# A decoder block on one core: weights repacked into load order, two more Strassen chunks, block sums and pooling products issued later

## The chip, the core and the metric

The kernel runs on one core of a Trainium2 chip. The metric is the time of one execution on the device in microseconds (us); a median of several runs is compared. The engines are TensorE (PE, with its weight loads as PEld), VectorE (DVE), ScalarE (ACT), GpSimd (POOL) and SyncE (SP, which here only issues DMAs).

## The reference

One decoder block for a sequence of T = 256 rows of D = 2048 features, all float32. A normalized input `z` is projected once by `w_in` (2048 x 11280); the result is split into the inputs of a pooling mixer, of a chunked gated linear attention (GLA) and of two branch gates.

```python
z = rms_norm(x, norm_mix_pre)
p, q, k, v, low, r, gates = split_combined(z @ w_in)     # 1024, 1024, 1024, 2048, 16, 2048, 2 x 2048
y = pool_mixer(p, w_pool, pool_scale)     # per group: trailing mean (window 2, 4, 8, 16) minus token, then 256 x 256
o = rms_norm_per_head(gla_chunked(q, k, v, log_a)) * silu(r)
ga, gb = sigmoid(gates + b_branch_gates)
m = ga * (y @ w_branch_a) + gb * (o @ w_branch_b)
x = x + rms_norm(m @ w_out, norm_mix_post)
h = rms_norm(x, norm_ffn_pre)
f = silu(h @ w_ffn_gate) * (h @ w_ffn_up)                # 5632 wide
out = x + rms_norm(f @ w_ffn_down, norm_ffn_post)
```

(The names are shortened; the arithmetic is that of the reference.) Nearly all work is the product of 256 rows with some 280 MB of weights, each of which is read once.

## The kernel before

**Jobs, steps and units.** Every weight matrix is cut into chunks of 512 output columns (CW). One chunk is a `Job` (L207); the list of jobs stands at L876 to L913 in the order of computing: p (2 chunks), r (4; the first is 528 wide and takes the 16 columns of `low` along), q and k (2 each), branch_a (4), v (4), gates (8), branch_b (4), out (4), and then the FFN in three parts of up to four chunks: gate and up alternating, then down (4). A `Step` is 256 weight rows of a chunk, loaded as one `raw` of 512 KB from SyncE's queue (L256). A *unit* is a step or a part (below) with its matmuls; the loop at L978 issues one unit after another, and this loop is what sets the order on every engine.

**Precision.** A weight tile is split into a high half `wh` (ScalarE, L265) and a low half `wl` = raw - wh (VectorE, L269), and each product takes three matmuls: high x high (L296), high x low (L297), low x high (L298). A step is 12 matmuls of 512 columns. Jobs p, q and k are computed transposed ("across", L285 to L287, 24 matmuls of 256 columns a step).

**Strassen chunks.** A job with `fast=True` computes its first eight 128-row weight tiles (two block rows of 512 KB x 2) by a Strassen-Winograd scheme in seven `Part`s of 12 matmuls with 256 columns (L357 to L359), and the rest, four steps for a 2048-row weight, as before. Its weight blocks are loaded at L943 into `blocks` tiles. Sums of weight blocks are made in place: part r5 by an accumulating DMA from GpSimd's queue (L329), q6, q7 and q4 on VectorE (L318, L320, L322); parts are split at L333 (ScalarE) and L337 (VectorE). Parts q1, r5, q6, q7 are "early": `merged` (L231) puts them between the last units of the job before. Two subtractions on 256 columns (L369) finish the products. Before the change 39 chunks are Strassen chunks: gates 1, 3, 5, 7, branch_b 1, 3, out 1, 2, and in the FFN gate and up chunks except number 0, and down except the last.

**Block sums of activations.** A Strassen chunk needs sums of the activations' blocks too, once for each activation (h, o, m, h2, f of each part). `combine` (L173) returns them as six pieces with 12 operations on VectorE (L182, L188, L193; 128 x 512 each) and four on ScalarE (L187).

**What sets the order.** `prepare_to` (L946) runs loads, block sums and splits for the next units: up to BUFS = 4 splits ahead of TensorE; raws in RAWS = 3 buffers, blocks in BLOCKS = 3. Small work is queued in `bg`; the loop takes one entry after each unit (L994). `after(n, f)` (L375) puts work into `soon`, which is looked at before each unit (L982): entries run while the *first* of them is due, so an entry that is not due holds up those behind it. At the end of an up chunk (L827) f = silu(gate) * up is made; after chunk 1 of a part the six pieces of `combine` go to the front of `bg` three units later, one per unit from there; the two transposes of f's halves (`to_operand`, after 1 and 2 units) stand behind that entry in `soon`.

**Pooling mixer.** `pool_group` (L450) runs from `bg` for each of four groups: running sums on VectorE, then the load of the group's `w_pool` (ScalarE's queue, L467), four matmuls (L471) and the split into `yT`, all at once.

## Time and profile before

| | |
|---|---|
| median of 3 runs | 1521.74 us (1520.41 to 1523.68) |
| profiled execution | 1520.68 us, span 1518.9 us |
| TensorE busy | 98% of the span |
| VectorE, ScalarE, GpSimd busy | 77%, 58%, 5% |
| read from device memory | 282.74 MB, 188 GB/s over the span |
| clock granted to TensorE | 0.998 of full speed |

A row like `L337 DVE TENSOR_TENSOR wl<-blocks,wh ... x273 | 331.7, 1221 | 79.6 <-ACT wh L333 76.5` is a group of instructions: line, engine, operation, output <- inputs by the program's names, shape, count, then busy us and mean ns of one, then the engine's idle time just before these instructions and what ended most of it. A row of a window gives start and end in us, its length, each engine's busy us (and count), the granted clock, the mean share of DMA engines in use and GB/s. In a timeline each row is a start, a duration, an instruction, and in brackets the idle time before it with what ended it. Ends of matmuls are modelled, so that a run of short matmuls is better read by its count in a full window than by the duration of one.

### The profile page before, as it was taken

The page shows a single profiled execution, that of the slowest core. Times are in us where ns is not written, and L with a number is a line of the kernel's source. Part 1 is how long each engine was busy: PE and PEld are TensorE (multiplying, and loading weights), DVE is VectorE, ACT ScalarE, POOL GpSimd, SP SyncE. Part 2 cuts the span into 40 slices and gives each one's busy share as a digit, 9 for nine tenths or more (in the row PEclk, how much of TensorE's full clock was granted, in tenths as well). Part 3 has the DMA queues.
Part 4 walks back from the last instruction along what each step waited for, and adds up shares of the span by engine and source line. Part 5 has one row for each costly group of instructions (what it writes and reads, how often), then busy time and mean ns, then how long its engine had stood idle before and what let it go on. Part 6 is the DMA issues. An engine that isn't in the chain of part 4 may idle for free.

```text
span 1518.9 us, 22882 instructions
## 1 busy us (share of the span) xinstructions
PE 1487.0 (98%) x8904; PEld 1306.4 (86%) x8904; DVE 1173.0 (77%) x1303; ACT 879.3 (58%) x1136; POOL 80.3 (5%) x89
## 2 busy tenths in 40 slices
PE   8999999999999999999999999999999999999997
PEld 8888999888888888888878989998998889888886
DVE  5665445785578866787768899888889898888997
ACT  6367333555455555554656666666666666666663
POOL 2000000000000000000000000000000000000001
PEclk9999999999999999999999999999999999999999
DMA  9856665445547776657865777778876777787664
GB/s 293 241 158 194 193 182 179 126 137 155 166 125 221 236 236 196 213 168 255 259 184 153 213 196 231 218 225 224 236 212 199 226 217 222 226 236 222 186 181 139
DMA packets 167630, 306.79 MB, mean 202 GB/s; under 512 B 9773, under 2 KB 30977, under 8 KB 167265
## 3 DMA queue, kind: packets, MB, share of 16 engines
q1 hardware_dynamic: 144176, 279.15, 57.7%
q0 software_dynamic: 22128, 24.92, 10.7%
q8 instruction: 70, 1.15, 0.3%
q10 hardware_dynamic: 1216, 1.25, 0.3%
q14 instruction: 40, 0.32, 0.1%
HBM read 282.74 MB, written 2.10 MB: 188 GB/s over the span
## 4 chain that ended last, share of the span: by engine, by line
PE 80%; DVE 10%; issue 4%; DMA 4%; ACT 2%; POOL 0%; SPq 0%; DVEq 0%; ACTq 0%; POOLq 0%
PE acc L296 16%; PE acc L297 16%; PE acc L298 16%; PE ac L358 4%; PE ac L357 4%; PE ac L359 4%; PE acc L358 3%; PE acc L357 3%; PE acc L359 3%; DVE wl L269 3%; PE acc L287 2%; PE acc L286 2%; PE acc L285 2%; DMA raw<-in_w_in_dram 2%; DVE wl L337 2%
## 5 line engine op out<-in xcount | busy, mean ns | idle before, releaser
L269 DVE TENSOR_TENSOR wl<-raw,wh 128x1024 fp32r<-128x1024 f32 (+1 forms) x364 | 444.6, 1223 | 211.5 <-ACT wh L265 209.5
L265 ACT ACTIVATE wh<-raw 128x1024 fp32r<-128x1024 f32 (+1 forms) x364 | 385.0, 1059 | 382.0 <-PE acc L298 171.3
L337 DVE TENSOR_TENSOR wl<-blocks,wh 128x1024 fp32r<-128x1024 f32 x273 | 331.7, 1221 | 79.6 <-ACT wh L333 76.5
L333 ACT ACTIVATE wh<-blocks 128x1024 fp32r<-128x1024 f32 x273 | 286.6, 1058 | 139.7 <-PE acc L298 62.8
L329 POOL DMA_DIRECT2D blocks<-blocks x39 | 50.7, 1301 | 792.4 <-DMA blocks<-in_w_ffn_gate_dram 163.1
L359 PE MATMUL ac<-wh,x 128*128 128x256 f32 x312 | 87.3, 280 | 0.0
L357 PE MATMUL ac<-wh,x 128*128 128x256 f32 x312 | 87.2, 279 | 0.0
L358 PE MATMUL ac<-wl,x 128*128 128x256 f32 x312 | 87.1, 279 | 0.0
L297 PE MATMUL acc<-wl,h22h 128*128 128x512 f32 x176 | 69.9, 397 | 5.2 <-DVE wl L269 5.2
L296 PE MATMUL acc<-wh,h22h 128*128 128x512 f32 x176 | 69.8, 397 | 0.2 <-ACT wh L265 0.2
L298 PE MATMUL acc<-wh,h23l 128*128 128x512 f32 x176 | 69.3, 394 | 0.0
L297 PE MATMUL acc<-wl,h23h 128*128 128x512 f32 x176 | 69.3, 394 | 0.0
L296 PE MATMUL acc<-wh,h23h 128*128 128x512 f32 x176 | 69.2, 393 | 0.0
L298 PE MATMUL acc<-wh,h22l 128*128 128x512 f32 x176 | 69.2, 394 | 0.0
L357 PEld LDWEIGHTS ac<-wh,x 128*128 128x128 f32 x312 | 58.6, 188 | 2.6
L358 PEld LDWEIGHTS ac<-wl,x 128*128 128x128 f32 x312 | 58.6, 188 | 2.4
L359 PEld LDWEIGHTS ac<-wh,x 128*128 128x128 f32 x312 | 58.8, 189 | 0.3 <-DVE x L188 0.2
L297 PE MATMUL acc<-wl,h3h 128*128 128x512 f32 (+1 forms) x128 | 49.8, 389 | 0.9 <-DVE wl L269 0.9
L296 PE MATMUL acc<-wh,h2h 128*128 128x512 f32 (+1 forms) x128 | 49.9, 390 | 0.0
L297 PE MATMUL acc<-wl,h2h 128*128 128x512 f32 (+1 forms) x128 | 49.7, 388 | 0.0
L298 PE MATMUL acc<-wh,h3l 128*128 128x512 f32 (+1 forms) x128 | 49.7, 388 | 0.0
L298 PE MATMUL acc<-wh,h2l 128*128 128x512 f32 (+1 forms) x128 | 49.7, 388 | 0.0
(540 smaller groups left out, 4123.6 us busy)
## 6 DMA issues: line engine op xcount, KB each, us to landing
raw<-in_w_in_dram SPq DMA_DIRECT2D x152, 512.0 KB, 3.7
raw<-in_w_ffn_gate_dram SPq DMA_DIRECT2D x48, 512.0 KB, 4.9
raw<-in_w_ffn_up_dram SPq DMA_DIRECT2D x48, 512.0 KB, 4.5
blocks<-in_w_ffn_down_dram SPq DMA_DIRECT2D x44, 512.0 KB, 5.0
raw<-in_w_ffn_down_dram SPq DMA_DIRECT2D x44, 512.0 KB, 4.9
blocks<-in_w_ffn_gate_dram SPq DMA_DIRECT2D x40, 512.0 KB, 4.8
blocks<-in_w_ffn_up_dram SPq DMA_DIRECT2D x40, 512.0 KB, 4.8
blocks<-blocks POOLq DMA_DIRECT2D x39, 512.0 KB, 6.7
```

Source lines behind the costliest of these rows:

```text
L265: act.activation(self.hi[self.s], self.raw, AF.Copy)
L269: dve.tensor_tensor(self.lo[self.s], self.raw, f32(self.hi[self.s]), op=ALU.subtract)
L285: pe.matmul(dst, wh, ah, start=first and c % 2 == 0, stop=False)
L296: pe.matmul(ps, ah, hi[:, i, cs], start=first, stop=False, skip_group_check=j.fast)
L297: pe.matmul(ps, ah, lo[:, i, cs], start=False, stop=False, skip_group_check=j.fast)
L298: pe.matmul(ps, al, hi[:, i, cs], start=False, stop=last, skip_group_check=j.fast)
L329: pool.dma_start(self.block((0, 1)), self.block((0, 0)), accum_op=ALU.add)
L333: act.activation(self.hi, self.src, AF.Copy)
L337: dve.tensor_tensor(self.lo, self.src, f32(self.hi), op=ALU.subtract)
L357: pe.matmul(dst, ah, wh, start=i == 0 and p in ("q1", "r5"), stop=False, skip_group_check=True)
L358: pe.matmul(dst, ah, wl, start=False, stop=False, skip_group_check=True)
L359: pe.matmul(dst, al, wh, start=False, stop=i == 3 and p in EARLY, skip_group_check=True)
```

## The change

1. **Layout.** The host lays the seven big weights out as one-dimensional arrays in load order: each 512 KB load is contiguous, 4 KB for each of the 128 partitions (before: two rows of 2 KB). A pair of block loads now brings the left and the right 256 columns of four weight tiles (before: two tiles of 512 columns each), so each block is contiguous in its `blocks` tile. `w_pool` is laid out likewise. The `raw`, `wh` and `wl` tiles have the width of the job instead of 528 columns.
2. **Block sums of f.** The six pieces go out 5 units apart in FFN parts 0 and 1, and 2 units apart in part 2, starting at the next unit, through `after`. `soon` is now a list in which each due entry runs, whatever stands ahead of it.
3. **Pooling product.** The load of `w_pool`, the four matmuls and the split of y come three units after the group's differences.
4. **Strassen chunks.** Gates 2, 4, 5, 6, 7 (before 1, 3, 5, 7) and out 0, 1, 2 (before 1, 2): 41 instead of 39.

```diff
+WEIGHTS = ("w_in", "w_branch_a", "w_branch_b", "w_out", "w_ffn_gate", "w_ffn_up", "w_ffn_down")
...
+        yield "gates", n, "w_in", 0, kt, OFF_GA + n * CW, CW, n in (2, 4, 5, 6, 7)
+    for n in range(4):
+        yield "b", n, "w_branch_b", 0, kt, n * CW, CW, n in (1, 3)
+    for n in range(4):
+        yield "out", n, "w_out", 0, kt, n * CW, CW, n < 3
...
+def packed(name, w):
...
+    out = []
+    for _, _, which, k0, kt, c0, width, fast in plan():
+        if which != name:
+            continue
+        rows = w[0, k0 * P:(k0 + kt) * P, c0:c0 + width].reshape(kt, P, width)
+        if fast:
+            for b in range(2):
+                blocks = rows[b * 4:b * 4 + 4].reshape(4, P, 2, HW)
+                out.append(blocks.transpose(2, 1, 0, 3).ravel())
+            rows = rows[4 * FAST:]
+        out.append(rows.reshape(-1, GK, P, width).transpose(0, 2, 1, 3).ravel())
+    return np.concatenate(out)
...
+        def combine_slowly(self, first, step):
+            for i, f in enumerate(self.combine()):
+                after(first + i * step, f)
...
         def load(self):
             j = self.j
-            r0 = (j.k0 + self.g * GK) * P
-            raw = wp.tile([P, GK, CW + RANK], F32, tag="raw", name=nm("raw"), bufs=RAWS)
-            s = self.s = (slice(None), slice(None), slice(0, j.width))
-            sync.dma_start(raw[s], j.w[r0:r0 + GK * P, j.c0:j.c0 + j.width].rearrange("(g p) c -> p g c", p=P))
-            self.raw = raw[s]
+            n = GK * P * j.width
+            self.raw = wp.tile([P, GK, j.width], F32, tag="raw", name=nm("raw"), bufs=RAWS)
+            sync.dma_start(self.raw, j.w[j.at + self.g * n:j.at + (self.g + 1) * n]
+                           .rearrange("(p g c) -> p g c", p=P, g=GK))
...
-            rows, cols_ = which
-            return self.j.blocks[rows][:, :, cols_ * HW:(cols_ + 1) * HW]
+            return self.j.blocks[which[0]][:, which[1]]
...
-                    bg.popleft()()
+                    (bg.popleft() if bg else soon.pop(0)[1])()
...
-    soon = deque()
+    soon = []
...
+        after(3, lambda: pool_product(g, d))
+
+    def pool_product(g, d):
         wt = two(scratch())
-        act.dma_start(wt, w_pool[0, g].rearrange("(k p) c -> p k c", p=P))
+        act.dma_start(wt, w_pool[g])
...
-                after(3, lambda: bg.extendleft(reversed(fa[part].combine())))
+                after(3, lambda: fa[part].combine_slowly(0, 5 if part < 2 else 2))
...
-            project(OFF_GA + which * D, n, gate_done(which, n), fast=n % 2 > 0)
-        jobs.append(Job(w_branch_b[0], lambda: oT["o"], KT, n * CW, yb_done(n), fast=n % 2 > 0))
-        jobs.append(Job(w_out[0], lambda: mix["m"], KT, n * CW, out_done(n), tail=3 * (n == 3), fast=n in (1, 2)))
...
+    for kind, n, name, k0, kt, c0, width, fast in plan():
+        jobs.append(Job(source[name], at[name], kt, width, fast, **kinds[kind](n)))
+        at[name] += kt * P * width
...
-            tile_ = blk.tile([P, 4, CW], F32, tag="blocks", name=nm("blocks"))
+            tile_ = blk.tile([P, 2, 4, HW], F32, tag="blocks", name=nm("blocks"))
             j.blocks.append(tile_)
+            n = 4 * P * HW
             for i in range(2):
-                r0 = (j.k0 + rows_ * 4 + i * 2) * P
-                sync.dma_start(tile_[:, i * 2:i * 2 + 2], j.w[r0:r0 + 2 * P, j.c0:j.c0 + CW]
-                               .rearrange("(g p) c -> p g c", p=P))
+                at = j.at + (rows_ * 2 + i) * n
+                sync.dma_start(tile_[:, i], j.w[at:at + n].rearrange("(p k c) -> p k c", p=P, k=4))
...
-        while soon and soon[0][0] <= 0:
-            soon.popleft()[1]()
-        for waiting in soon:
-            waiting[0] -= 1
+        due = [x for x in soon if x[0] <= 0]
+        soon = [[n_ - 1, f] for n_, f in soon if n_ > 0]
+        for _, f in due:
+            f()
```

The line numbers of the changed kernel are about 50 higher: `wh` and `wl` of a step are made at L316 and L320, `wl` of a part at L387, the pooling product stands at L524, and the VectorE lines of `combine` at L230, L236 and L241.

**TensorE at the first pooling product.** `qt_537` holds the first group's differences, `acc_511` and `acc_512` are p's chunk 1. Before:

```order
L287 MATMUL acc_511<-h0l,wh_429 128x256
L285 MATMUL acc_511<-h0h,wh_429 128x256
L286 MATMUL acc_511<-h0h,wl_431 128x256
L471 MATMUL tr_545<-qt_537,scr_543 128x256 x4
L287 MATMUL acc_511<-h0l,wh_429 128x256
L285 MATMUL acc_512<-h0h,wh_429 128x256
```

After (between these two pieces of the order 67 rows of the same chunk have gone ahead of it):

```order
L336 MATMUL acc_512<-h1h,wh_507 128x256
L337 MATMUL acc_512<-h1h,wl_509 128x256
L338 MATMUL acc_512<-h1l,wh_507 128x256
L524 MATMUL tr_649<-qt_537,scr_647 128x256 x4
L336 MATMUL acc_511<-h2h,wh_545 128x256
L337 MATMUL acc_511<-h2h,wl_547 128x256
```

The product stood inside the first unit of the chunk; now it stands three units later, before the rows that use `wh_545`, the split that was called `wh_556` before.

**VectorE at the block sums of f in FFN part 0.** `f01h`, `f01l`, `f00h`, `f00l` are halves of f, `fx` a block sum's low half, `scr` its scratch; `wl` are low halves for TensorE. Before:

```order
L168 TENSOR_TENSOR f01l<-tr_8080,f01h 128x512
L337 TENSOR_TENSOR wl_8110<-blocks_7821,wh_8108 128x1024
L182 TENSOR_TENSOR scr_8106<-f01h,f01l 128x512
L320 TENSOR_TENSOR blocks_7821<-blocks_7821 128x4x256
L193 TENSOR_TENSOR scr_8106<-scr_8104,scr_8106 128x512
L269 TENSOR_TENSOR wl_8132<-raw_8128,wh_8130 128x2x512
L188 TENSOR_TENSOR fx_8072<-scr_8106,fx_8071 128x512
L182 TENSOR_TENSOR scr_8146<-f00h,f00l 128x512
L337 TENSOR_TENSOR wl_8151<-blocks_7821,wh_8149 128x1024
L193 TENSOR_TENSOR scr_8104<-scr_8146,scr_8104 128x512
L269 TENSOR_TENSOR wl_8173<-raw_8169,wh_8171 128x2x512
L188 TENSOR_TENSOR fx_8072<-scr_8104,fx_8071 128x512
```

After:

```order
L216 TENSOR_TENSOR f01l<-tr_8175,f01h 128x512
L368 TENSOR_TENSOR blocks_7941<-blocks_7941,blocks_8112 128x1024
L320 TENSOR_TENSOR wl_8199<-raw_8195,wh_8197 128x1024
L230 TENSOR_TENSOR scr_8230<-f01h,f01l 128x512
L387 TENSOR_TENSOR wl_8226<-blocks_7941,wh_8224 128x1024
L370 TENSOR_TENSOR blocks_7941<-blocks_7941 128x1024
L320 TENSOR_TENSOR wl_8249<-raw_8245,wh_8247 128x1024
L241 TENSOR_TENSOR scr_8230<-scr_8228,scr_8230 128x512
L387 TENSOR_TENSOR wl_8265<-blocks_7941,wh_8263 128x1024
L320 TENSOR_TENSOR wl_8284<-raw_8280,wh_8282 128x1024
L419 TENSOR_TENSOR acc_8209<-ac_8208,u_8298 128x256
L387 TENSOR_TENSOR wl_8303<-blocks_8112,wh_8301 128x1024
```

Before, six of these twelve rows are operations of `combine`, one or two between every pair of low halves; now two of twelve are, and the ten others are splits and sums of weights and the output subtraction.

**VectorE at the end of branch_b.** `x_5906` (after: `x_5983`) is a block sum of o, `gb` and `ya` finish a branch_b chunk. Before, out chunk 0 is an ordinary chunk and the low halves that follow are those of its steps:

```order
L188 TENSOR_TENSOR x_5906<-scr_6026,x_5905 128x512
L322 TENSOR_TENSOR blocks_5677<-blocks_5677,blocks_5598 128x4x256
L269 TENSOR_TENSOR wl_6073<-raw_6069,wh_6071 128x2x512
L369 TENSOR_TENSOR acc_5947<-ac_5945,u_6088 128x256
L337 TENSOR_TENSOR wl_6093<-blocks_5677,wh_6091 128x1024
L732 TENSOR_TENSOR gb_4964<-gb_4964,acc_5853 128x512
L732 TENSOR_TENSOR gb_4965<-gb_4965,acc_5854 128x512
L733 TENSOR_TENSOR ya_2674<-ya_2674,gb_4964 128x512
L733 TENSOR_TENSOR ya_2675<-ya_2675,gb_4965 128x512
L337 TENSOR_TENSOR wl_6116<-blocks_5677,wh_6114 128x1024
```

After, low halves of early parts of out chunk 0 (`wl_6177` and `wl_6219`, from `blocks_5891`) stand there, between those of branch_b chunk 3 (from `blocks_5737`):

```order
L236 TENSOR_TENSOR x_5983<-scr_6086,x_5982 128x512
L372 TENSOR_TENSOR blocks_5737<-blocks_5737,blocks_5658 128x1024
L419 TENSOR_TENSOR acc_6010<-ac_6008,u_6149 128x256
L785 TENSOR_TENSOR gb_4965<-gb_4965,acc_5916 128x512
L785 TENSOR_TENSOR gb_4966<-gb_4966,acc_5917 128x512
L387 TENSOR_TENSOR wl_6154<-blocks_5737,wh_6152 128x1024
L786 TENSOR_TENSOR ya_2674<-ya_2674,gb_4965 128x512
L786 TENSOR_TENSOR ya_2675<-ya_2675,gb_4966 128x512
L387 TENSOR_TENSOR wl_6177<-blocks_5891,wh_6175 128x1024
L387 TENSOR_TENSOR wl_6193<-blocks_5737,wh_6191 128x1024
L216 TENSOR_TENSOR m2l<-tr_6198,m2h 128x512
L387 TENSOR_TENSOR wl_6219<-blocks_5891,wh_6217 128x1024
```

More of the change, by code (lines that the diff above doesn't have):

```diff
@@ L904, in tile_hybrid_block @@
-    chunks = DFF // CW
-    for part in range(3):
-        ms = range(part * 4, min(part * 4 + 4, chunks))
-        for m in ms:
-            jobs.append(Job(w_ffn_gate[0], lambda: h2["h"], KT, m * CW, ffn_gate_done(m), head=4 * (m == 0), fast=m > 0))
-            jobs.append(Job(w_ffn_up[0], lambda: h2["h"], KT, m * CW, ffn_up_done(m), fast=m > 0))
-        for n in range(4):
-            tail = part == 2 and n == 3
-            jobs.append(Job(w_ffn_down[0], lambda part=part: fa[part], 4 * len(ms), n * CW, down_done(part, n),
-                            k0=part * 16, tail=4 * tail, fast=not tail))
+    kinds = {
+        "p": lambda n: dict(lhs=lambda: hT, done=pool_done(n), across=True),
+        "r": lambda n: dict(lhs=lambda: hT, done=r_done(n)),
+        "q": lambda n: dict(lhs=lambda: hT, done=qk_done("q", n), across=True),
+        "k": lambda n: dict(lhs=lambda: hT, done=qk_done("k", n), across=True),
+        "a": lambda n: dict(lhs=lambda: yT, done=ya_done(n)),
+        "v": lambda n: dict(lhs=lambda: hT, done=v_done(n)),
+        "gates": lambda n: dict(lhs=lambda: hT, done=gate_done(*divmod(n, 4))),
+        "b": lambda n: dict(lhs=lambda: oT["o"], done=yb_done(n)),
+        "out": lambda n: dict(lhs=lambda: mix["m"], done=out_done(n), tail=3 * (n == 3)),
+        "gate": lambda m: dict(lhs=lambda: h2["h"], done=ffn_gate_done(m), head=4 * (m == 0)),
+        "up": lambda m: dict(lhs=lambda: h2["h"], done=ffn_up_done(m)),
+        "down": lambda pn: dict(lhs=lambda: fa[pn[0]], done=down_done(*pn), tail=4 * (pn == (2, 3))),
+    }
@@ L1012, in _constants, with _laid_out @@
     return {"ident": ident, "mask": np.concatenate(m, axis=1).astype(np.int32), "count": counts}
+def _laid_out(name, a):
+    import numpy as np
+    if name in WEIGHTS:
+        return packed(name, a)
+    if name == "w_pool":
+        a = a[0].reshape(4, 2, P, 2 * P).transpose(0, 2, 1, 3)
+    return np.ascontiguousarray(a)
 def kernel(**inputs):
@@ L1023 @@
     arrays, args = {}, []
-    for name, a in [(n, _np.ascontiguousarray(inputs[n])) for n in _INS] + list(_constants().items()):
+    for name, a in [(n, _laid_out(n, _np.asarray(inputs[n]))) for n in _INS] + list(_constants().items()):
         arrays[f"in_{name}_dram"] = a
```

56 lines of the change are left out of this document (28 added, 28 removed).

## The prediction, made before the changed kernel was run

> **What bounds the kernel now.** I read the page's head first, then the chain of waits, then the waits of TensorE, then stretches of time where TensorE is not full.
>
> ```profile
> span 1518.9 us, 22882 instructions
> PE 1487.0 (98%) x8904; PEld 1306.4 (86%) x8904; DVE 1173.0 (77%) x1303; ACT 879.3 (58%) x1136; POOL 80.3 (5%) x89
> PE 80%; DVE 10%; issue 4%; DMA 4%; ACT 2%; POOL 0%; SPq 0%; DVEq 0%; ACTq 0%; POOLq 0%
> ```
>
> TensorE bounds it. It is busy for 1487.0 of 1518.9 us, so all waits together are 31.9 us: no edit that only removes waits can bring more than 2.1%. The kernel gets faster in two ways only, fewer matmul microseconds or fewer of these 31.9. The next rows name the engine that TensorE waits for (columns: waiter, releaser, total us, times, longest).
>
> ```profile
> PE acc L297 <- DVE wl L269: 6.1, 4, 1.7
> PE acc L358 <- DVE wl L337: 2.6, 3, 0.9
> PE tr L471 <- issue: 2.1, 1, 2.1
> PE tr L471 <- DVE qt L465: 1.5, 1, 1.5
> ```
>
> Most of it is VectorE: a low half (wl) that isn't there in time, 8.7 us in seven waits, and the pool mixer's product (L471), 3.6 us in two. Where these lie is seen in stretches (columns: start and end, length, busy us of PE, PEld, DVE, ACT, POOL, clock, DMA share, GB/s).
>
> ```profile
> 40.00:50.00 10.00, 6.33 (x45) 5.74 (x44) 6.15 (x15) 3.79 (x5) 0.00 (x0) 1.00 1.04 340
> 490.00:500.00 10.00, 9.10 (x52) 7.57 (x52) 9.91 (x12) 5.49 (x9) 0.00 (x0) 1.00 0.47 122
> 890.00:910.00 20.00, 17.40 (x109) 15.22 (x108) 20.00 (x26) 14.00 (x21) 1.29 (x1) 1.00 0.58 145
> 930.00:950.00 20.00, 20.00 (x130) 17.97 (x129) 17.73 (x19) 12.93 (x17) 1.29 (x1) 1.00 0.72 204
> 950.00:970.00 20.00, 20.00 (x130) 18.09 (x129) 16.68 (x15) 13.02 (x17) 1.30 (x1) 1.00 0.79 226
> 1150.00:1170.00 20.00, 17.40 (x105) 15.10 (x104) 20.00 (x27) 13.89 (x19) 1.29 (x1) 1.00 0.58 144
> 1410.00:1430.00 20.00, 17.40 (x101) 14.93 (x101) 20.00 (x26) 13.21 (x18) 1.29 (x1) 1.00 0.58 147
> 1450.00:1480.00 30.00, 28.14 (x193) 25.50 (x192) 28.43 (x30) 19.28 (x28) 1.88 (x2) 1.00 0.57 158
> ```
>
> The three 17.40s are the places where the block sums of f are made, once in each FFN part: VectorE is busy 20.00 of 20.00 and TensorE loses 2.60 us each time. An ordinary Strassen stretch (930 to 970) leaves VectorE 2.27 and 3.32 us idle and TensorE loses nothing.
>
> **Pooling product (term A).** It moves 67 TensorE rows later; nothing is removed. In 40 to 50 TensorE idles 3.67 us, and both waits of the table stand there. The rows of TensorE, VectorE and ScalarE there say why (start, duration, instruction, idle time before it):
>
> ```profile
> 43.38 1.99 PE L471 MATMUL tr<-qt,scr 128*128 128x256 f32 x8 [1.53 <-DVE qt L465]
> 49.90 1.32 PE L471 MATMUL tr<-pt,scr 128*128 128x256 f32 x5 [2.14 <-issue]
> ...
> 43.17 0.15 DVE L465 TENSOR_TENSOR qt<-pt 128x2 f32<-128x2 f32 x1
> 46.37 1.23 DVE L269 TENSOR_TENSOR wl<-raw,wh 128x1024 fp32r<-128x1024 f32 x1 [2.38 <-ACT wh L265]
> 49.64 0.15 DVE L465 TENSOR_TENSOR pt<-qt,pt 128x6 f32<-128x6 f32 x1
> 45.28 1.06 ACT L265 ACTIVATE wh<-raw 128x1024 fp32r<-128x1024 f32 x1 [3.95 <-DMA raw<-in_w_in_dram]
> ```
>
> The pooled differences are ready at 43.3 and 49.8, held back in VectorE's order behind a wl whose raw load is late (ScalarE waits 3.95 us for it). TensorE stands at the first product from 43.38 − 1.53 = 41.85 and at the second from 49.90 − 2.14 = 47.76. One 256-column matmul takes 0.118 us (next part), so 67 rows are 7.9 us: the first product is reached near 49.5, the second near 54, both later than their operands by 4 us or more. What is late next is that wl itself, ready at 46.37 + 1.23 = 47.60; TensorE, freed of the product, reaches it only after 67 to 71 rows from 41.6, near 49.6. So the next wait doesn't take its place, with 2 us to spare. The load of w_pool is issued from ScalarE's queue later too, behind nothing new. **A = −3.6**, bounds −3.7 (all idle of the window) and −2.0 (the 2 us of slack gone).
>
> **Gates (term B).** Before, gate chunk 3 is a Strassen chunk and its early parts fall on the block sums of o: row 490 to 500, VectorE 9.91 of 10, TensorE idle 0.90. After, chunk 3 is ordinary, which needs fewer low halves. **B = −0.9**, bounds −0.9 and +1.0 (four Strassen chunks in a row from 4 to 7; the rows from 930 to 970 show that such a row keeps pace by itself).
>
> **Two more Strassen chunks (term C).** TensorE alone in two stretches, one with only 512-column matmuls, one with only 256-column ones:
>
> ```profile
> 112.00:160.00 48.00, 48.00 (x208) 1.00 0.66 188
> 188.00:248.00 60.00, 60.00 (x509) 1.00 0.65 185
> ```
>
> That is 0.2308 and 0.1179 us a matmul. In a chunk 48 of the former become 84 of the latter: 11.08 − 9.90 = 1.18 us less. **C = −2.35** for two.
>
> **What they cost VectorE (term D).** Each adds three low halves (seven parts replace four steps), three block sums and two half-width output subtractions; ScalarE gets three more high halves, POOL one accumulating transfer, SP no more bytes.
>
> ```profile
> L337 DVE TENSOR_TENSOR wl<-blocks,wh 128x1024 fp32r<-128x1024 f32 x273 | 331.7, 1221 | 79.6 <-ACT wh L333 76.5
> L322 DVE TENSOR_TENSOR blocks<-blocks,blocks 128x1024 f32<-128x1024 f32 x39 | 47.7, 1224 | 1.1
> L369 DVE TENSOR_TENSOR acc<-ac,u 128x256 f32<-128x256 f32 x78 | 33.1, 424 | 0.0
> 660.00:680.00 20.00, 20.00 (x117) 17.40 (x116) 20.00 (x26) 12.67 (x17) 0.00 (x0) 1.00 0.29 91
> 680.00:700.00 20.00, 19.64 (x103) 16.37 (x102) 16.57 (x20) 9.83 (x12) 1.30 (x1) 1.00 0.85 279
> 700.00:720.00 20.00, 20.00 (x110) 17.08 (x110) 15.09 (x15) 10.13 (x12) 0.00 (x0) 1.00 0.80 259
> ```
>
> 6 × 1.22 + 2 × 0.42 = 8.2 us of VectorE a chunk. At the gates it lies in ordinary stretches. At out chunk 0 it does not: its early parts now stand behind 660 to 680, where VectorE is already full with the block sums of the mixed branches. Between 680 and 700 fall two early low halves and two sums, 4.9 us, on 3.43 us of idle: 1.4 us late; the rest of the 8.2 meets the 4.91 idle of 700 to 720. **D = +1.4**, bounds 0 (TensorE's operands made ahead) and +4.9 (none of that idle usable).
>
> **Block sums of f spread (terms E and F).** No instruction is removed. One combination has 12 VectorE operations:
>
> ```profile
> L193 DVE TENSOR_TENSOR scr<-scr,scr 128x512 f32<-128x512 f32 x28 | 19.1, 683 | 0.1
> ```
>
> 12 × 0.683 = 8.2 us. A unit of work is 12 matmuls of 256 columns in a part, or of 512 in a step: (7 × 1.41 + 4 × 2.77) / 11 = 1.91 us. Before, one of six pieces runs per unit, so 8.2 us fall into 11.5 us, in which the idle of 930 to 970 (5.59 in 40) provides 1.6: 6.6 us too much, of which TensorE lost 2.6, so what was prepared ahead carried 4.0. In parts 0 and 1 a piece now comes every 5 units: 30 units are 57 us with 8.0 us of idle, 0.2 too much, well inside 4.0. The waits vanish: **E = −5.2** for two, bounds −5.2 and −2.0 (the idle of the rows is not where a piece falls). In part 2 the pieces are 2 units apart: 12 units, 23 us, 3.2 idle, 5.0 too much, 1.0 beyond what is ahead. **F = 1.0 − 2.6 = −1.6**, bounds −2.6 and 0.
>
> **Layout (term G).** Bytes and numbers of transfers stay; each weight load's row in a partition is one piece of 4 KB instead of 2 KB, and the accumulating transfer's too. No row shows a 4 KB piece. A contiguous source does nothing for ScalarE's own reading, and the loads are mostly in time:
>
> ```profile
> L265 ACT ACTIVATE wh<-raw 128x1024 fp32r<-128x1024 f32 x356 | 376.3, 1059 | 370.3 <-PE acc L298 171.3 <-PE acc L287 59.5 <-DMA raw<-in_w_in_dram 38.2
> L333 ACT ACTIVATE wh<-blocks 128x1024 fp32r<-128x1024 f32 x273 | 286.6, 1058 | 139.7 <-PE acc L298 62.8 <-issue 23.4 <-DVE blocks L320 18.4
> 0.00:20.00 20.00, 15.09 (x102) 13.56 (x103) 8.43 (x17) 13.80 (x32) 5.59 (x16) 1.00 0.85 281
> ```
>
> Only the beginning and the end could use quicker loads: up to 2.5 of the 4.9 us idle in 0 to 20 and the 1.9 idle in 1450 to 1480. In the crowded row 40 to 50 the engines are taken up at 340 GB/s and 1.04 share, so there it is a rate, elsewhere mostly a latency. **G = 0**, bounds −4.4 and +1.0. The Trainium skill, "DMA: Bandwidth & Descriptors", section "Why small descriptors are slow (HBM only)", gives about 3 fixed cycles a packet beside one for each 32 bytes; an estimate from it is 131 cycles for 4 KB against 2 × 67, 2.2% less. By it, too, G is a few tenths of a microsecond at the start.
>
> Sum: −3.6 − 0.9 − 2.35 + 1.4 − 5.2 − 1.6 + 0 = −12.25. From the profiled execution's 1520.68 (its span 1518.9 and 1.8 around it, 1.1 below the median shown, 1521.74): **1508.4**.
>
> **Rivals.** (1) The backlog only moves. VectorE's work is the same, and the pieces of f fall on places where a low half was just in time. Against it: the idle in 930 to 970 is a wait for ScalarE, in front of the work. For it: TensorE's cover there is thin, since 6.6 of excess already cost 2.6. Price: E −2 instead of −5.2, F 0, D +3: 1508.4 + 3.2 + 1.6 + 1.6 = 1514.8.
>
> (2) The late raw load takes the pool product's place. If the 2 us of slack are not there, the wl wait of 2.38 us on VectorE reaches TensorE: 1508.4 + 2.4 = 1510.8. For it: ScalarE's 3.95 us on the raw.
>
> (3) The layout decides. The loads become so much quicker that the starting waits for raw (2.5), the end (1.9) and the last f wait (1.0) go: 1508.4 − 5.4 = 1503.0. The Trainium skill, "Perfetto Trace Analysis", section "DMA Optimizations", says that going from 2 KB to 4 KB pieces can raise throughput dramatically where the kernel is bound by DMA. The trace bears that out little: 281 GB/s with TensorE waiting at the start, but 204 and 226 GB/s with no wait from 930 to 970.
>
> (4) Slower: VectorE becomes the bound. The two chunks add 16.4 us to it. It decides from the point where VectorE's idle near a new chunk falls under 8.2; at out 0 the rows from 660 to 720 have 0 + 3.43 + 4.91 = 8.34. If those waits can't be filled, TensorE follows VectorE through both chunks: +16.4 in place of B and D, with E and F at 0: 1520.7 − 3.6 − 2.35 + 16.4 = 1531. For it: the thin 0.1 us. Against it: nothing forces the 8.2 into three windows, since low halves are made up to 4 us ahead.
>
> **How the numbers follow.** Forecast 63%, rival 1 16%, rival 2 7%, rival 3 9%, rival 4 5%. The predicted time is the forecast's, 1508.4. Its own bounds give 1503 to 1514; the range reaches to rivals 1 and 3 and to D's upper bound with the others as taken: 1501 to 1516. About 0.2%, 3 us, is what a measurement can tell from no change. Faster 0.92 (all but rival 4 and a tail of rival 1), same 0.04, slower 0.04.
>
> **What would show it.** A: no TensorE wait at the pool product (L524 now) and none on wl near 50. C: 72 more matmuls, TensorE's busy time down by about 2. E: in the stretches of f TensorE at 20.00 of 20 in parts 0 and 1, about 1 us lost in part 2. D: TensorE idle of 1 to 2 us behind branch_b chunk 3. G: the same landing times of loads within a few per cent, and the same idle in 0 to 20. It would be wrong if low halves (L320, L387 now) cost TensorE as much as before somewhere else, or if waits in the first 50 us went with quicker loads.

## The result

The changed kernel takes 1500.76 us in the median (1499.66 to 1501.28) against 1522.42 for the kernel before: a ratio of 0.9858, 95% interval 0.9841 to 0.9875. A second set of runs gave 1500.74 against 1521.61 (0.9860, 0.9846 to 0.9875). That is 21 us less, where 12.25 had been worked out, and 0.24 us under the lower end of the stated range. The profiled spans, 1518.9 and 1497.9, differ by 21.0 us.

The head of the profile page of the changed kernel, its chain of waits by engine, and then all waits of TensorE that add up to 0.5 us or more (columns as before):

```profile
span 1497.9 us, 23015 instructions
PE 1481.0 (99%) x8976; PEld 1306.7 (87%) x8976; DVE 1185.1 (79%) x1319; ACT 887.3 (59%) x1150; POOL 64.8 (4%) x91
PE 90%; DVE 4%; issue 3%; DMA 2%; ACT 1%; POOL 0%; SPq 0%; DVEq 0%; POOLq 0%; ACTq 0%
```

```profile
PE tr L179 <- DMA x<-in_x_dram: 1.8, 3, 1.2
PE acc L347 <- ACT h20h L218: 1.1, 3, 0.6
PE tr L151 <- DVE scr L148: 1.1, 1, 1.1
PE acc L338 <- DVE h3l L219: 0.7, 1, 0.7
PE acc L347 <- ACT wh L316: 0.7, 2, 0.6
PE ac L407 <- ACT wh L383: 0.5, 1, 0.5
...
PE acc L348 <- DVE wl L320: 0.2, 1, 0.2
...
PE ac L408 <- DVE wl L387: 0.2, 1, 0.2
```

TensorE's idle time fell from 31.9 to 16.9 us. The waits for a low half went from 8.7 us to 0.4, those of the pooling product (L524 now) are gone, and VectorE's share of the chain of waits fell from 10% to 4%. TensorE's busy time fell by 6.0 us with 72 more matmuls, which the prediction had put at about 2. The median landing times of the FFN's block loads, which it had expected to stay within a few per cent, went from 4.8 to 5.0 us down to 4.3 to 4.4.

The stretches of the changed kernel that answer to those shown of before (the pooling product, the block sums of f in parts 0, 1 and 2, the end):

```profile
40.00:60.00 20.00, 20.00 (x160) 19.59 (x159) 13.38 (x22) 9.16 (x11) 0.90 (x1) 1.00 0.93 319
...
870.00:890.00 20.00, 20.00 (x130) 17.93 (x129) 18.04 (x21) 12.41 (x16) 0.85 (x1) 1.00 0.71 213
890.00:910.00 20.00, 20.00 (x129) 18.04 (x128) 19.96 (x23) 14.58 (x19) 0.85 (x1) 1.00 0.72 219
1128.00:1148.00 20.00, 20.00 (x132) 18.02 (x131) 18.43 (x21) 13.04 (x18) 0.85 (x1) 1.00 0.65 196
1390.00:1410.00 20.00, 20.00 (x127) 17.95 (x126) 20.00 (x24) 14.53 (x20) 0.85 (x1) 1.00 0.69 202
1410.00:1430.00 20.00, 19.77 (x131) 17.55 (x131) 19.80 (x23) 12.97 (x18) 0.85 (x1) 1.00 0.67 212
1430.00:1460.00 30.00, 28.65 (x193) 25.79 (x192) 29.48 (x31) 19.18 (x28) 1.42 (x2) 1.00 0.56 170
```

TensorE is full where it had lost 3.67 us and, in parts 0 and 1, 2.60 us; in part 2 it still loses 0.23 us in 1410 to 1430. VectorE is still at 19.96 and 20.00 of 20 in two of these rows, and TensorE does not wait: a full VectorE is not yet a late one.

To see where the time went I cut both traces into stages by the start of the first matmul of each stage and took the difference of these starts. "f" is from the first gate chunk of an FFN part to the first matmul with f of that part (in parts 1 and 2 from the last matmul with the part before).

| stage | before, us | after, us | difference |
|---|---|---|---|
| start to p's chunk 1 | 38.26 | 36.74 | −1.5 |
| p's chunk 1 (pooling product) | 30.39 | 25.96 | −4.4 |
| r | 95.59 | 95.58 | 0.0 |
| q and k | 90.99 | 89.94 | −1.05 |
| branch_a | 65.87 | 65.91 | 0.0 |
| v and gates | 283.51 | 281.31 | −2.2 |
| branch_b and out | 178.43 | 176.32 | −2.1 |
| f, parts 0, 1, 2 | 173.42, 158.37, 115.48 | 170.04, 154.81, 112.18 | −3.4, −3.6, −3.3 |
| down, parts 0 and 1; rest | 100.73, 100.73, 87.14 | 100.85, 100.86, 87.35 | +0.45 |

The profiles of the kernels below repeat most of these stages to a few hundredths where their code is the same (q and k: 90.98 or 90.99 in every one with the old tile width). Three do not. The first stage lies between 36.5 and 38.5 us in all of them whatever the layout, so its −1.5 is no effect of the change that the profiles can show. P's chunk 1 takes 29.8 to 31.2 us in the kernel before and in the three below that add one other part of the change, so what the later product brings there is known to about 1 us. Branch_b and out scatters by about 1 us either way.

### The profile page after: what moved, and what is told of

The parts are those of the page before. It is cut to its first block, busy times and chain, and to the rows that moved or that the text cites. A ratio compares the mean times of both kernels' runs of the same rounds, so it can differ in the third digit from the quotient of the medians.

```text
span 1497.9 us, 23015 instructions
## 1 busy us (share of the span) xinstructions
PE 1481.0 (99%) x8976; PEld 1306.7 (87%) x8976; DVE 1185.1 (79%) x1319; ACT 887.3 (59%) x1150; POOL 64.8 (4%) x91
## 4 chain that ended last, share of the span: by engine, by line
PE 90%; DVE 4%; issue 3%; DMA 2%; ACT 1%; POOL 0%; SPq 0%; DVEq 0%; POOLq 0%; ACTq 0%
PE acc L347 17%; PE acc L349 17%; PE acc L348 17%; PE ac L408 5%; PE ac L407 5%; PE ac L409 5%; PE acc L409 4%; PE acc L407 4%; PE acc L408 4%; PE acc L338 3%; PE acc L336 3%; PE acc L337 3%; PE tr L662 1%; DMA raw<-in_w_in_dram 1%; PE tr L179 1%
## 5 line engine op out<-in xcount | busy, mean ns | idle before, releaser
L316 ACT ACTIVATE wh<-raw 128x1024 fp32r<-128x1024 f32 (+1 forms) x356 | 376.7, 1059 | 360.3 <-PE acc L349 186.3
L320 DVE TENSOR_TENSOR wl<-raw,wh 128x1024 fp32r<-128x1024 f32 (+1 forms) x356 | 435.1, 1224 | 183.1 <-ACT wh L316 181.5
L387 DVE TENSOR_TENSOR wl<-blocks,wh 128x1024 fp32r<-128x1024 f32 x287 | 348.9, 1222 | 73.9 <-ACT wh L383 70.4
L383 ACT ACTIVATE wh<-blocks 128x1024 fp32r<-128x1024 f32 x287 | 301.7, 1058 | 143.3 <-PE acc L349 57.1
L409 PE MATMUL ac<-wh,x 128*128 128x256 f32 x336 | 94.1, 280 | 0.0
L408 PE MATMUL ac<-wl,x 128*128 128x256 f32 x336 | 94.1, 280 | 0.0
L407 PE MATMUL ac<-wh,x 128*128 128x256 f32 x336 | 94.0, 280 | 0.0
L379 POOL DMA_DIRECT2D blocks<-blocks x41 | 35.4, 864 | 811.8 <-DVE wl L320 329.7
L407 PEld LDWEIGHTS ac<-wh,x 128*128 128x128 f32 x336 | 63.1, 188 | 2.6
L409 PEld LDWEIGHTS ac<-wh,x 128*128 128x128 f32 x336 | 63.6, 189 | 0.0
L372 DVE TENSOR_TENSOR blocks<-blocks,blocks 128x1024 f32<-128x1024 f32 x41 | 50.2, 1224 | 1.1
L368 DVE TENSOR_TENSOR blocks<-blocks,blocks 128x1024 f32<-128x1024 f32 x41 | 50.1, 1222 | 0.9
L370 DVE TENSOR_TENSOR blocks<-blocks 128x1024 f32<-128x1024 f32 x41 | 50.0, 1219 | 0.1
```

Source lines behind the costliest of these rows:

```text
L316: act.activation(self.hi, self.raw, AF.Copy)
L320: dve.tensor_tensor(self.lo, self.raw, f32(self.hi), op=ALU.subtract)
L368: dve.tensor_tensor(b12, b12, b22, op=ALU.add)
L372: dve.tensor_tensor(b21, b21, b12, op=ALU.add)
L383: act.activation(self.hi, self.src, AF.Copy)
L387: dve.tensor_tensor(self.lo, self.src, f32(self.hi), op=ALU.subtract)
```

## The experiments

**Each part alone.** Theory A: the terms of the prediction stand and the layout, taken at 0, carries the missing 8.7 us. Theory B: the other terms were sized too small. The four kernels are the kernel before with one part of the change each.

```diff
 layout_only: the arrays, loads and tiles of the change; 39 Strassen chunks, sums and product as before
 pool_only
+        after(3, lambda: pool_product(g, d))
+    def pool_product(g, d):
         wt = two(scratch())
 spread_only
-                after(3, lambda: bg.extendleft(reversed(fa[part].combine())))
+                after(3, lambda: fa[part].combine_slowly(0, 5 if part < 2 else 2))
 ...                                       and the new queue: soon as a list
 chunks_only
-        project(OFF_GA + which * D, n, gate_done(which, n), fast=n % 2 > 0)
+        project(OFF_GA + which * D, n, gate_done(which, n), fast=which * 4 + n in (2, 4, 5, 6, 7))
-    ... out_done(n), tail=3 * (n == 3), fast=n in (1, 2)
+    ... out_done(n), tail=3 * (n == 3), fast=n < 3
```

Expected of the layout:

> The kernel before with the new weight layout and the tile widths that go with it, nothing else (39 Strassen chunks, product and block sums as before). The change gave 21.0 us of span where the terms summed to 12.25; 8.7 are unaccounted for. Theory A, the layout carries them: span 8 to 9 us shorter than 1518.9, with the TensorE waits on late raws near 12.6 and 35.9 gone or halved and the f waits (0.9 and 1.7 us per part) shorter too. Theory B, the other terms were sized too small and the layout gives about the first wait alone: 1 to 3 us shorter, f waits as before.

Of the pooling product:

> The kernel before with only the pooling product issued three units later. Theory A: 3.6 us less span, as in the prediction. Theory B (gaps between starts of matmuls were longer than the idle that the windows show): 4.4 us less. If the late raw load takes the product's place (rival 2): 1 to 2 us less, with a TensorE wait on wl near 50.

Of the block sums of f:

> The kernel before with only the block sums of f spread (5, 5 and 2 units apart, and the list without head blocking). Theory A: 6.8 us less span (2.6 + 2.6 + 1.6). Theory B: 9.3 us less (3.3 + 3.4 + 2.6), the f windows full in parts 0 and 1. If the backlog only moves (rival 1): about 2 us less.

Of the Strassen chunks:

> The kernel before with only the 41 Strassen chunks (gates 2, 4, 5, 6, 7 and out 0, 1, 2). Theory A: 1.85 us less span (-2.35 matmuls, -0.9 gates, +1.4 at out 0, where TensorE idles 1 to 2 us behind branch_b chunk 3). Theory B: VectorE's 8.2 us at out 0 cost nothing: 3.3 to 4 us less. If VectorE becomes the bound (rival 4): longer than before.

Against 1521.2 us of the kernel before on that chip: layout 1520.86 (ratio 0.9996, 0.9987 to 1.0005), product 1517.45 (0.9973, 0.9963 to 0.9983), block sums 1514.07 (0.9950, 0.9936 to 0.9965), chunks 1518.69 (0.9982, 0.9973 to 0.9992). Theory A falls: the layout alone is no difference that can be measured. It leaves the f waits as they were, while the spread alone removes them; the same two stretches, first in the kernel with the layout only, then in the one with the spread only:

```profile
890.00:910.00 20.00, 17.68 (x114) 15.46 (x112) 19.97 (x25) 14.01 (x21) 0.86 (x1) 1.00 0.50 148
1150.00:1170.00 20.00, 17.40 (x109) 15.06 (x108) 20.00 (x26) 14.02 (x21) 0.86 (x1) 1.00 0.52 151
```

```profile
890.00:910.00 20.00, 20.00 (x126) 17.94 (x126) 20.00 (x22) 13.69 (x18) 1.29 (x1) 1.00 0.80 227
1150.00:1170.00 20.00, 20.00 (x126) 17.90 (x125) 19.97 (x24) 14.24 (x20) 1.22 (x1) 1.00 0.79 213
```

By stages: the product is worth 4.2 us in its stage against the profile of the kernel before (3.8 by the medians); the spread −3.0 in each of the three f stretches and +0.7 at the end; the chunks −1.05 at the gates. The layout is worth −1.05 in q and k, but +2.4 in v and gates. Theory B holds in part only, since the four add up to −0.3 − 3.8 − 7.1 − 2.5 = −13.7 us: together the parts bring some 7 us more.

**Each part taken back from the changed kernel.** The same edits in reverse, one at a time.

> The changed kernel with the old weight layout: later product, spread block sums and 41 Strassen chunks on the kernel before. One at a time the four parts gave -0.3 (layout), -3.8, -7.1 and -2.5 us, -13.7 in all, where all together gave some -21. Theory A, the missing 7 us are the layout's in company of the other edits (quicker loads where more blocks are asked for): about 13 us below the kernel before, 7 to 8 above the changed one. Theory B, the layout has no part in it: within 1 us of the changed kernel.

> The changed kernel with the 39 Strassen chunks of before. If the missing 7 us come from layout and chunks together (waits at the gates and at the out chunks that vanish only with both): 9 to 10 us above the changed kernel. If chunks are worth what they gave alone: 2.5 above it.

> The changed kernel with the block sums of f one unit apart and the old queue. If the layout and the spread work together: 12 to 14 us above the changed kernel. If the spread is worth what it gave alone: 7 above it, all of it in the three f stretches.

> The changed kernel with the pooling product at once. If it is worth what it gave alone: 3.8 us above the changed kernel, all of it before 70 us. If the layout shortens the wait on the late raw: 2 to 3.

| taken back | median, us | above 1500.76 | worth alone |
|---|---|---|---|
| layout | 1504.45 | 3.7 | 0.3 |
| chunks | 1507.18 | 6.4 | 2.5 |
| spread | 1510.64 | 9.9 | 7.1 |
| product | 1506.15 | 5.4 (1503.0 to 1508.45; span 3.4) | 3.8 |

By these medians each is worth more in company. The stages do not bear that out for two of them: the product is worth 2.9 us in its stage, and the spread 3.1 to 3.2 in each f stretch, with the rest of its 9.9 in the two stages that scatter, the first one and branch_b and out. They show one place where two parts depend on each other far beyond the scatter, v and gates:

| v and gates, us | old layout | new layout |
|---|---|---|
| gates 1, 3, 5, 7 | 283.51, 283.56, 283.67 | 285.95, 286.48, 286.50 |
| gates 2, 4, 5, 6, 7 | 282.22, 282.46 | 281.31 (five profiles), 281.99 |

With the old set the new layout costs 2.4 to 3 us, with the new set it brings about 1. So the move of the gates is worth 1.05 to 1.3 us with the old layout and 5 with the new.

**Four more changes of the changed kernel.** Tile width, spacing of the pieces, out 0, and two Strassen chunks more.

```diff
 wide_splits
-            self.hi = wp.tile([P, GK, self.j.width], F32R, tag="wh", name=nm("wh"))
+            self.hi = wp.tile([P, GK, CW + RANK], F32R, tag="wh", name=nm("wh"))   # and self.lo; 512 columns used
 steps_1_2_3
-                after(3, lambda: fa[part].combine_slowly(0, 5 if part < 2 else 2))
+                after(3, lambda: fa[part].combine_slowly(0, part + 1))
 no_out0
-        yield "out", n, "w_out", 0, kt, n * CW, CW, n < 3
+        yield "out", n, "w_out", 0, kt, n * CW, CW, n in (1, 2)
 more_fast
-        ... n in (2, 4, 5, 6, 7)          # gates
+        ... n in (1, 2, 4, 5, 6, 7)
-        ... n in (1, 3)                   # branch_b
+        ... n > 0
-                after(3, lambda: bg.extendleft(reversed(mix["m"].combine())))
+                after(3, lambda: mix["m"].combine_slowly(0, 2))
```

> The changed kernel with wh and wl tiles of a step 528 columns wide again, of which 512 are used (raw stays as loaded). In every kernel with the new layout the stage of q and k (32 steps, weights as the stationary operand) is 1.05 us shorter, in every kernel without it not: 0.117 against 0.118 us a matmul. Theory A, the distance between rows of the wh and wl tiles does it: the 1.05 us come back (and 0.5 in p), all else as in the changed kernel, some 1.5 us above it. Theory B, the transfers do it (4 KB pieces): within 0.3 us of the changed kernel in that stage.

The kernel takes 1503.63 us, and the stage of q and k is back at 90.99. TensorE alone in a stretch of q and k, in the kernel before, in the changed one, and in the changed one with 528-column tiles:

```profile
186.00:244.00 58.00, 58.00 (x492) 1.00 0.67 188
```

```profile
186.00:244.00 58.00, 58.00 (x497) 1.00 0.59 186
```

```profile
186.00:244.00 58.00, 58.00 (x492) 1.00 0.61 187
```

0.1179, 0.1167 and 0.1179 us a matmul: five more matmuls in the same 58 us when rows of wh and wl stand 512 instead of 528 columns apart, whatever the transfers do. The f stretches also go back, to 170.38, 155.38 and 112.57 us; without the layout they are 170.38, 155.38 and 112.58. So in q, k and the f stretches, taking back the tile width takes back all that the new layout brought. In q and k that holds in every profile. In the f stretches it is not the whole account: the changed kernel with other sets of Strassen chunks keeps the narrow tiles and still takes up to 170.24, 155.30 and 112.55 us there, so part of these gains hangs on something that was not isolated. In r, mostly matmuls of 512 columns, the narrow tiles are 0.2 us slower (95.35 to 95.58 in the kernels with the later product).

> The changed kernel with the six pieces of f's block sums 1 unit apart in FFN part 0, 2 in part 1, 3 in part 2 (changed kernel: 5, 5, 2). By the VectorE budget of the prediction (8.2 us of sums, 0.27 us idle a unit, 4.0 us prepared ahead): TensorE loses 2.6 us in part 0, 1.0 in part 1, nothing in part 2; 3.6 in the first two parts against the changed kernel, less what its part 2 loses. If it was the queue that held up f's transposes and not the spacing: part 0 loses under 1 us too.

1502.63 us. Against the changed kernel the f stage is 1.7 us longer in part 0 (1 unit apart), 0.9 in part 1 (2 units) and equal in part 2 (3 units). Before, pieces one unit apart cost 3.0. So both edits work: the new queue brings a bit under half of it in part 0, the spacing the rest. That the queue does so by letting the transposes of f go ahead is likely from the code, but was not tested by itself. The stretch of part 0 in this kernel, with the 1.4 us that TensorE loses:

```profile
880.00:900.00 20.00, 18.65 (x114) 16.38 (x113) 20.00 (x25) 14.02 (x20) 0.85 (x1) 1.00 0.55 161
```

> The changed kernel with out chunk 0 ordinary. By the prediction (C: -1.18, D: +1.4) out 0 as a Strassen chunk is worth +0.2: within 0.5 us of the changed kernel, a shade faster. If VectorE's extra 8.2 us there are made ahead and cost nothing: 1.2 above it. If the ordinary out 0 also keeps the waits behind branch_b chunk 3 (0.3 to 2 us in four profiles): 1.5 to 3 above it.

1502.64 us, 1.9 above the changed kernel. Over all profiles, branch_b and out together take 176.1 to 178.0 us with out 0 as a Strassen chunk (13 profiles, mean 177.15) and 178.0 to 180.3 with out 0 ordinary (6 profiles, mean 179.1).

> The changed kernel with two Strassen chunks more (gates 1, branch_b 2) and the block sums of the mixed branches m spread 2 units apart. If VectorE has room: 2.4 us below the changed kernel. If VectorE is the bound there (each chunk adds 8.2 us; at branch_b and out it has under 8 us idle in 60): 2 to 8 us above it, with TensorE waiting for wl.

1503.28 us, 2.5 above the changed kernel. The two chunks, with m's block sums spread in the same edit, are too much: at the gates TensorE loses 1.5 us, and beside branch_b VectorE is full over two rows in which TensorE loses 1.6. At the gates VectorE is not full (15.59 of 20): it idles 3.0 us shortly before TensorE's wait, behind ScalarE, which waits there for raws that land 7.3 and 6.6 us after their issue at 484.74 and 487.98, beside an accumulating transfer issued at 484.81.

```profile
480.00:500.00 20.00, 18.46 (x83) 14.74 (x82) 15.59 (x21) 10.32 (x14) 1.43 (x2) 1.00 0.75 227
660.00:680.00 20.00, 19.22 (x119) 16.67 (x118) 20.00 (x27) 12.78 (x17) 0.00 (x0) 1.00 0.63 195
680.00:700.00 20.00, 19.21 (x115) 16.31 (x114) 19.93 (x23) 12.38 (x16) 0.85 (x1) 1.00 0.78 231
```

**What the layout does at the gates.** The changed kernel again, then with the old set of gates, then with the raws in two pieces of 2 KB.

```diff
 old_gates
-        ... n in (2, 4, 5, 6, 7)
+        ... n % 2 > 0
 raw_2k
-        out.append(rows.reshape(-1, GK, P, width).transpose(0, 2, 1, 3).ravel())
+        out.append(rows.ravel())
-                           .rearrange("(p g c) -> p g c", p=P, g=GK))
+                           .rearrange("(g p c) -> p g c", p=P, g=GK))
```

> The changed kernel once more, unchanged, beside the two below. Both theories: 20 to 22 us below the kernel before; by stages as in its first profile within 0.5 us, except the first 40 us, where kernels with the same code there have differed by up to 2 us.

> The changed kernel with the old set of Strassen chunks among the gates (1, 3, 5, 7), out 0 kept. Theory A, the new layout makes the old set worse (283.5 us without it in the stage of v and gates, 286 with it; new set 282.3 and 281.3): the stage takes 285.5 to 286.5, the kernel 4 to 5 us above the changed one. Theory B, that was the doing of the other chunk sets or chance: 283.5, 2.2 above it.

> The changed kernel with the raws contiguous as 512 KB but row by row, so that each partition takes two pieces of 2 KB as before; blocks and tiles as in the changed kernel. Theory A, the 4 KB pieces of the raws bring what the layout brings beyond the tile width (some 2.7 of 3.7 us): 2 to 3 us above the changed kernel, spread over gates and FFN. Theory B, piece size is worth 2% of a transfer that is mostly latency: within 0.7 us of the changed kernel in each stage behind the first 40 us.

The repeat has the first profile's stages to 0.2 us. The old gates cost 6.1 us (1506.83), with 286.48 in the stage. Raws in pieces of 2 KB cost 0.7 (1501.48, within the scatter of 1500.74): 0.75 more in v and gates, 0.2 to 0.4 in branch_b and out, nothing in the FFN. Three more kernels take one part of the layout back from the one with the old gates; the third keeps the contiguous loads but puts the blocks into tiles of four rows of 512 columns again, so that the accumulating transfer moves pieces of 1 KB.

```diff
 old_gates_old_blocks
-            tile_ = blk.tile([P, 2, 4, HW], F32, tag="blocks", name=nm("blocks"))
+            tile_ = blk.tile([P, 4, CW], F32, tag="blocks", name=nm("blocks"))
-            return self.j.blocks[which[0]][:, which[1]]
+            return self.j.blocks[which[0]][:, :, which[1] * HW:(which[1] + 1) * HW]
 ...                                       and the host's order: a load brings two tiles of 512 columns
```

> The old set of gates in the changed kernel (stage of v and gates 286.5 us; 283.5 with the old layout) with wh and wl tiles 528 wide. Theory A, tile width (TensorE reaches the stage 1 us earlier, its loads don't): 283.5 to 284.5. Theories B and C: 286 to 287.

> The old set of gates in the changed kernel with raws in pieces of 2 KB. Theory B, the raws' larger pieces hold up the small bias load that shares the engines with them and what follows: 283.5 to 284.5. Theories A and C: 286 to 287.

> The old set of gates in the changed kernel with the blocks in tiles of four rows of 512 columns as before (loads still contiguous in 4 KB, the accumulating transfer again in pieces of 1 KB). Theory C, the blocks' order (a pair of loads now brings left and right halves) or the quicker accumulating transfer does it: 283.5 to 284.5. Theories A and B: 286 to 287.

The stage takes 285.21, 286.28 and 283.86 us, the kernels 1507.57, 1507.08 and 1506.49 against 1523.09 of the kernel before on that chip. As ratios (0.9901, 0.9898 and 0.9894, against 0.9902 with the old gates alone) these can't be told apart, so what follows rests on the stage. It is the blocks (2.6 of the 3 us), with a share of the tile width (1.3, perhaps because TensorE arrives later there). The trace shows how. ScalarE and VectorE beside the early parts of gate 3, old gates with the new blocks:

```profile
473.09 1.06 ACT L316 ACTIVATE wh<-raw 128x1024 fp32r<-128x1024 f32 x1 [2.56 <-PE acc L349]
...
474.19 1.23 DVE L320 TENSOR_TENSOR wl<-raw,wh 128x1024 fp32r<-128x1024 f32 x1 [1.92 <-ACT wh L316]
...
486.56 0.50 PE L348 MATMUL acc<-wl,h2h 128*128 128x512 f32 x1 [1.94 <-DVE wl L320]
```

and with the old blocks:

```profile
470.46 1.06 ACT L316 ACTIVATE wh<-raw 128x1024 fp32r<-128x1024 f32 x1 [0.42 <-DMA raw<-in_w_in_dram]
...
471.69 1.22 DVE L320 TENSOR_TENSOR wl<-raw,wh 128x1024 fp32r<-128x1024 f32 x1
```

The raw of that low half is issued at 466.70 in the first and 466.19 in the second, each time within 0.6 us of the accumulating transfer (issued 466.11 and 465.81). With new blocks the transfer lands after 6.4 us and the raw after 6.3; with old blocks the transfer after 8.7 and the raw after 4.2. GpSimd's groups of the two kernels show the issue getting shorter:

```profile
L379 POOL DMA_DIRECT2D blocks<-blocks x40 | 34.8, 869 | 812.8 <-DVE wl L320 351.4 <-DVE blocks L368 162.0 <-DMA blocks<-in_w_out_dram 63.5
```

```profile
L379 POOL DMA_DIRECT2D blocks<-blocks x40 | 52.0, 1300 | 800.8 <-DVE wl L320 343.3 <-DVE blocks L368 178.5 <-DMA blocks<-in_w_out_dram 81.8
```

So the accumulating transfer now lands ahead of the raw instead of behind it. The same pair lands so in every profile with the old gates: after 6.2 to 6.6 and 6.2 to 6.5 us in the five with new blocks, after 7.4 to 8.7 and 4.1 to 4.2 in the four with old ones, whose stages take 285.2 to 286.5 and 283.5 to 283.9 us. VectorE then idles 1.92 us for that raw just before a stretch in which it is full with o's block sums and gate 3's parts, and the delay reaches TensorE undiminished, 1.94 us at 486.56 (the row names ScalarE's raw wait as one for a matmul; the raw landed at 472.99, 0.1 us before ScalarE began). That is not all of the 2.6 us. The rows from 476 to 487 and from 487 to 495 with new blocks, then the latter with old blocks:

```profile
476.00:487.00 11.00, 9.06 (x51) 7.54 (x50) 11.00 (x15) 6.64 (x9) 0.00 (x0) 1.00 0.30 97
487.00:495.00 8.00, 8.00 (x36) 6.73 (x35) 8.00 (x11) 3.86 (x5) 0.00 (x0) 0.79 0.41 114
```

```profile
487.00:495.00 8.00, 7.08 (x42) 5.91 (x41) 7.91 (x9) 5.58 (x8) 0.00 (x0) 1.00 0.44 122
```

With new blocks the granted clock is 0.79 in this profile over the 8 us behind the wait (and in the one with raws of 2 KB), worth 1.7 us, and with old blocks TensorE has a wait of 0.92 us there instead: 1.94 + 1.7 − 0.92 = 2.7. In the changed kernel with all 39 chunks of before the clock is at 1.00 there, and the first wait (1.9 us) is followed by a second of 1.0. So the raw's delay starts the loss, and what it adds up to differs from profile to profile. With the new set of gates VectorE has 9.54 and 9.31 of 10 in the rows from 470 to 490 and TensorE does not wait. What stays open is which property of the new blocks counts, their order in the loads or the length of the accumulating transfer's pieces: one kernel took both back.

## Why the prediction was wrong

The direction was right, and so was the mechanism of the later product and of the spread block sums. The sum came out too small: one term had the wrong sign, others were sized too small, and one part of the change was not costed.

- **A (pooling product), −3.6 predicted.** Alone −4.2 in its stage and −3.8 by the medians, in the change −4.4 with some 0.2 from the tile width of p. The step that sized it took the idle of the 40 to 50 row. Matmul ends are modelled in these rows: from one start to the next TensorE was 1.70 and 2.30 us behind its pace at the two products, 4.0 in all. The reading that both products were held back behind the late wl holds for the second alone: the first differences were ready at 43.32, before that wl began at 46.37. No late wl took the product's place, so rival 2 is out.
- **B and half of C (gates), −2.1 predicted.** −2.2 in the change, right by luck of two errors. With the old layout the move is worth 1.05 to 1.3; with the new one 5, of which the layout had first cost 2.4 to 3. The step from "Bytes and numbers of transfers stay" to G = 0 failed here: it asked what quicker transfers bring and not what they push back.
- **C and D at out 0, −1.18 + 1.4 = +0.2 predicted; about −1.9 measured.** This is the one term with a wrong sign. The failed step is "4.9 us on 3.43 us of idle: 1.4 us late". It charged VectorE's work to TensorE as soon as a 20 us window was full, and left out the 4.0 us prepared ahead with which term E reckons. In the changed kernel, which is some 9 us earlier here, the rows from 660 to 700 show VectorE at 19.96 and 19.46 and TensorE at 20.00. So C's 1.18 us come through whole. The stage is 1.7 us longer with out 0 ordinary, and the rest of that stays open: the waits behind branch_b for the transposes of the mixed branches come and go in both kinds of kernel (0.2 to 1.8 us with out 0 ordinary, 0 to 1.2 with out 0 as a Strassen chunk).

```profile
660.00:680.00 20.00, 20.00 (x134) 18.11 (x133) 19.96 (x24) 13.28 (x18) 0.00 (x0) 1.00 0.54 181
680.00:700.00 20.00, 20.00 (x131) 17.98 (x130) 19.46 (x23) 12.86 (x18) 0.90 (x1) 1.00 0.90 283
```

- **E (f, parts 0 and 1), −5.2 predicted.** −6.0 by the spread alone, −6.9 in the change; 0.8 of the difference is the window's idle again (start to start the waits of one part were 3.05 us, not 2.60), the rest goes when the tile width is taken back. The budget (work of the pieces, idle of a unit, what is prepared ahead) was right for 5 units. For pieces 1 unit apart it says 2.6, and 1.7 was measured with the new queue; for 2 units 1.0 against 0.9.
- **F (f, part 2), −1.6 predicted.** −3.0 in its stage, of which 0.7 comes back at the end: −2.3 by the spread alone. (The end takes 86.3 to 87.1 us in the five profiles without the spread and 87.0 to 88.7 with it.)
- **G (layout), 0 predicted.** Right for the layout alone (−0.3, within the scatter) and for the raws' pieces (0.7 at most). Wrong for the change, where taking the layout back costs 3.7 us: 1.05 in q and k and 0.3 to 0.6 in each f stretch go when the tile width is taken back, and about 1 lies at the gates. The tile width stands under "The change" and the prediction did not cost it at all. The first 40 us show no gain.

Stage by stage the 21.05 us of the two profiles are 8.8 more than the 12.25 worked out, and these are, roughly: 2.3 at out 0, 1.7 in E, 1.7 in F less 0.45 in the down parts and the end, 1.05 in q and k, 0.8 in A, 0.1 at the gates, and 1.5 in the first 40 us, which is scatter. The largest failed step is thus D. The range was too narrow as well: the bounds of the single terms add up to 1501.5 to 1521.2, not to the 1503 to 1514 called the forecast's own, and 1500.76 lies just outside even these.

Rival 3 comes nearest in time and is wrong in cause: the quicker loads it counted on, at the start and the end, brought nothing that can be seen. Of the rule that larger transfers can dramatically raise throughput where a kernel is bound by DMA (the Trainium skill, "Perfetto Trace Analysis", "DMA Optimizations") the runs show no more than 0.7 us in 1500 for the raws; this kernel, with TensorE busy 99% of the span, is not such a case. Rival 1 and rival 4 did not come about, though rival 4's mechanism, a full VectorE, is what the two further Strassen chunks run into beside branch_b.

## What to carry to other kernels

Size a wait from the distance between starts of instructions against their pace, not from the idle column of a window, and charge a busy helper engine only from the point where what it has prepared ahead is used up. A quicker transfer also changes who goes first on the shared DMA engines: just ahead of a stretch where an engine has no slack, that can cost more than the transfer saves. And look at the tile shapes that come along with a change of layout, since a tile 528 instead of 512 columns wide moved the pace of TensorE by 1% in q and k.

## What was not expected of the hardware

Matmuls of 256 columns with the split weights as the stationary operand take 0.1167 us when the rows of that tile stand 512 columns apart and 0.1179 when they stand 528 apart, in every profile of either kind. The issue of the accumulating transfer takes GpSimd 0.87 us with pieces of 4 KB and 1.30 with pieces of 1 KB, and beside the early parts of gate 3 its landing trades places with that of a load issued 0.3 to 0.6 us behind it: 6.4 and 6.3 us with the larger pieces, 8.7 and 4.2 with the smaller.
